# The residual of one half row of the last pair, added on TensorE in PSUM instead of by the store

## Chip, cores and metric

The kernel runs on one core of a Trainium2 chip. The metric is the device time of one execution in microseconds, the median of several runs. Lower is better. All times below are in microseconds unless marked ns.

## What is computed

One decoder layer on a sequence of 1024 tokens of width 1024, in fp32: a token-mixing sub-layer (attention and a gated recurrence), then a squared-ReLU MLP of width 4096. The end of it is what matters here:

```python
    h = rmsnorm(x, pre_w_mlp[l]) * (1.0 + sc2) + sh2
    u = jnp.square(jax.nn.relu(h @ w_up[l]))
    x = x + g2 * rmsnorm(u @ w_down[l], post_w_mlp[l])
```

So each row of the output is the residual x plus a row of the down projection, times a gate row (g2 times the norm's weight), times one number per row, the reciprocal root of the row's mean square. That number is known only when both halves of the row are complete.

## The kernel before

The 1024 rows are eight blocks of 128 rows (`tb` 0 to 7), each of two halves of 512 columns. A tile is 128x512 fp32, 256 KB. In the token-mixing part `out_proj` (L1045) computes the residual of the second sub-layer and stores it from GpSimd's queue (L1066). Thirteen of its sixteen tiles go straight into the output tensor `out`; three go to a scratch tensor in HBM, `x1d` (L1041), which the table `hold` (L1042) lists: block 3's second half and both halves of block 7.

Both MLP products are done in a block scheme with seven products per group instead of eight, each as three products of split fp32 operands. In the down projection a list of loads, `seq`, is worked through in order: `load_ahead` (L1320) issues loads some entries ahead from SyncE's queue, and `take` (L1327) hands out the next tile. The last three entries of `seq` are the residual tiles in `x1d` (L1318).

The last group of the down projection runs by row blocks `t` = 0 to 3, each of which completes two blocks of rows, t and t + 4. The loop over `order` (L1628) does t = 0, 1, 2 and the first three products of t = 3. Work on finished blocks is put off by some steps with `on` and done a step at a time: `square` (ScalarE squares a half with a running sum), `gated` (VectorE times the gate row), `root` (VectorE adds the two sums, GpSimd takes the power -0.5, tile `rrf`), `scaled` (ScalarE times that number, first the half `1 - half`, then `half`) and `onto_x` (L1619). The last is an adding store: GpSimd issues a DMA with `accum_op=add`, which adds the tile `acc` to what `out` holds, half 0 first. When a pair's second half is done, `half` is 0, so the scaling goes over half 1 and then half 0. Every engine works its own queue in the order in which the code records; a wait holds all that stands behind it on that engine.

`last_rows` (L1660) does what is left of t = 3: block a = 3 and block b = 7. TensorE's products go to the PSUM banks `pdlb`, `pdc`, `pda` and, last, `pdlx` in two parts of 256 columns. Block a's halves are multiplied by the gate row early (tiles `ga0` for half 0 and `ga` for half 1, L1686). After that:

- the root of block a (L1696), and for block b the sums, three squares (`finl`), the sum of them (`l_part`) and the root (`l_r`) on GpSimd
- `ga0`: scaled by block a's root on ScalarE (L1701) and stored by GpSimd as an adding store (L1706)
- `ga`: one VectorE instruction (times the root, plus the residual tile) and a plain store from SyncE (L1710)
- `gl` for both halves of block b: a VectorE instruction each and a plain store, from ScalarE's queue for half 0 and SyncE's for half 1 (L1713)

The program ends with a drain of each engine and a barrier, which the profile puts on L1781. All recorded operations pass through one helper and stand under L39.

Of the kernel before, what the change touches and what calls it, by code (L numbers as in the profile page):

```python
# [9 lines left out]
F32 = mybir.dt.float32  # L10
F32R = mybir.dt.float32r
I32 = mybir.dt.int32
AF = mybir.ActivationFunctionType
ALU = mybir.AluOpType
AX = mybir.AxisListType

P = 128
D = 1024
# [29 lines left out]
def hybrid_layer(ctx: ExitStack, tc: tile.TileContext, I, out, dbg=None):  # L48
    nc = tc.nc
    ACT, DVE, POOL, PE, SP = (Queue(tc, e) for e in (nc.scalar, nc.vector, nc.gpsimd, nc.tensor, nc.sync))  # L50
# [17 lines left out]
    small = ctx.enter_context(tc.tile_pool(name="small", bufs=2, side="right"))  # L68
# [3 lines left out]
    dram = ctx.enter_context(tc.tile_pool(name="dram", bufs=1, space=bass.MemoryType.DRAM))  # L72
# [19 lines left out]
    def tp_ps(name):  # L92
        return pb.tile([P, 512], F32, tag="b", name=name)

    def a_ps(name):
        return pa.tile([P, 512], F32, tag="aps", name=name)
# [18 lines left out]
    ident, cT, bT, prew1, prew2 = (tab[:, a:b] for a, b in ((0, P), (P, 136), (136, 184), (184, 192), (192, 200)))  # L115
# [922 lines left out]

    x2ctx = ExitStack()
    X2 = x2ctx.enter_context(tc.tile_pool(name="poolX2", bufs=1))  # L1040
    x1d = dram.tile([P, 3 * 512], F32, tag="x1d", name="x1d")  # L1041
    hold = {(3, 1): slice(0, 512), (7, 0): slice(512, D), (7, 1): slice(D, D + 512)}  # L1042
    xn2 = [None] * TB

    def out_proj(tb):  # L1045
# [106 lines left out]
    def flush():  # L1152
        for dst, src in pend:
            SP.dma_start(dst, src)
        pend.clear()
# [154 lines left out]
    for i, (g, n) in enumerate(stages):  # L1310
# [3 lines left out]
        if 10 <= i and gates:  # L1314
            entry_gate(*gates.pop(0))
        ends.append(len(seq))
    for i in range(3):
        seq.append((f"x1_{i}", lambda i=i: x1d[:, i * 512:i * 512 + 512], None))  # L1318

    def load_ahead():  # L1320
        while at["load"] < min(len(seq), at["use"] + (LEAD if at["load"] >= 16 else 4) + 1):
            k = at["load"]
            mk = (raw_, t_)[k % 2] if k < 16 else (raw_, t_, t_, raw_, t_, raw_, t_, t_)[k % 8]
            rawt[k] = load_raw(mk, seq[k][0], seq[k][1]())
            at["load"] += 1

    def take():  # L1327
        load_ahead()
        raw = rawt.pop(at["use"])
        at["use"] += 1  # L1330
        return raw

    def pump(count, limit=None):

        for _ in range(count):
            if at["use"] < (ends[-1] if limit is None else limit):
                k = at["use"]
                seq[k][2](take())
# [164 lines left out]
    def dmm(pst, g, n, t, first, cols=slice(0, 512)):  # L1503
        ps = GROUPS[g]
        for p in ps:
            (ah, al), (bh, bl) = (tuple(u[:, t * P:t * P + P] for u in su[p, n]), tuple(w[:, cols] for w in sw[p, n]))
            for x, (l, r) in enumerate(((ah, bh), (ah, bl), (al, bh))):
                PE.matmul(pst, lhsT=l, rhs=r, start=(first and p == ps[0] and x == 0), stop=(p == ps[-1] and x == 2),
                          skip_group_check=not first)

    def accum(tb, half, pst):
        if accs[tb][half] is None:
            accs[tb][half] = g_(f"acc{tb}_{half}")
            ACT.activation(accs[tb][half], pst, AF.Copy)
        else:
            DVE.tensor_tensor(accs[tb][half], pst, accs[tb][half], ALU.add)
# [77 lines left out]
    ssr, rr_, later = {}, {}, {}  # L1594

    def on(step, fn):
        later.setdefault(step, []).append(fn)

    def square(tb, half):
        if tb not in ssr:  # L1600
            ssr[tb] = small.tile([P, 2], F32, tag="ssf", name=f"ssf2{tb}")
        ACT.activation(a_ps(f"fin{tb}_{half}"), accs[tb][half], AF.Square, accum_out=ssr[tb][:, half:half + 1])

    def gated(tb, half):
        DVE.tensor_tensor(accs[tb][half], accs[tb][half], gw2[:, half * 512:half * 512 + 512], ALU.mult)
# [6 lines left out]
    def root(tb):  # L1612
        ss, rr_[tb] = (small.tile([P, 1], F32, tag=f"{n}1", name=f"{n}f{tb}") for n in ("ss", "rr"))
        root_of(rr_[tb], ss, ssr[tb][:, 0:1], ssr[tb][:, 1:2])

    def scaled(tb, half):
        ACT.activation(accs[tb][half], accs[tb][half], AF.Copy, scale=rr_[tb][:, 0:1])

    def onto_x(tb, halves=(0, 1)):  # L1619

        for half in halves:
            POOL.dma_start(out[tb * P:(tb + 1) * P, half * 512:half * 512 + 512], accs[tb][half], accum_op=ALU.add)
# [4 lines left out]
    bk = {}  # L1627
    for step, (_, t, k) in enumerate(order):  # L1628
        n = ORDER[k]
        key, first, th, half = PLAN[n]  # L1630
        flush()
        if first:
            bk[key, t] = (mm_ps if key == "a" else tp_ps)(f"pd{key}{g}_{t}")
        dmm(bk[key, t], g, n, t, first)
        while todo:
            todo.pop(0)()
        todo.append(lambda tb=t + 4 * th, half=half, pst=bk[key, t]: accum(tb, half, pst))
        for fn in later.pop(step, []):
            fn()
        if 2 <= step < 6:  # L1640
            pump(1)
        if k >= 3 and t < 3:
            tb = t + 4 * th
            on(step + 1, lambda tb=tb, half=half: square(tb, half))
            if k < 5:
                on(step + 3, lambda tb=tb, half=half: gated(tb, half))
            else:
                on(step + 3, lambda tb=tb: root(tb))
                on(step + 3, lambda tb=tb, half=half: gated(tb, half))
                for hf in (1 - half, half):  # L1650
                    on(step + 4, lambda tb=tb, hf=hf: scaled(tb, hf))
                on(step + 5, lambda tb=tb: onto_x(tb))
    nstep = len(order)

    def rest(step):
# [4 lines left out]
    def last_rows():  # L1660
        a, b, t = 3, 7, 3
        ss = small.tile([P, 3], F32, tag="ssl", bufs=1, name="ssl")
        one = {n: small.tile([P, 1], F32, tag="l_" + n, bufs=1, name="l_" + n) for n in ("part", "r")}
        h = [slice(0, 512), slice(512, D)]
        ba, bc, bb, bx = bk["a", 3], bk["c", 3], tp_ps("pdlb"), tp_ps("pdlx")
        gl = [m_(f"gl{half}") for half in range(2)]
        ga0, ga = m_("ga0"), m_("ga")

        def sq(acc, col, w=512):
            ACT.activation(a_ps("finl" + str(len(ssr)))[:, 0:w], acc, AF.Square, accum_out=col)  # L1670

        def add(dst, pst):
            DVE.tensor_tensor(dst, pst, dst, ALU.add)

        dmm(bb, g, 2, t, True)
        while todo:
            todo.pop(0)()
        rest(nstep)
        dmm(bc, g, 3, t, False)
        add(accs[a][0], bb)  # L1680
        square(a, 0)
        rest(nstep + 1)
        dmm(ba, g, 7, t, False)
        add(accs[a][1], bc)
        square(a, 1)
        DVE.tensor_tensor(ga0, accs[a][0], gw2[:, h[0]], ALU.mult)  # L1686
        DVE.tensor_tensor(ga, accs[a][1], gw2[:, h[1]], ALU.mult)
        rest(nstep + 2)
        acp = [accs[b][0][:, 256 * i:256 * i + 256] for i in range(2)]
        dmm(bx[:, 0:256], g, 4, t, True, slice(0, 256))  # L1690
        dmm(bx[:, 256:512], g, 4, t, True, slice(256, 512))
        for step in sorted(later):
            rest(step)
        add(accs[b][1], ba)
        sq(accs[b][1], ss[:, 0:1])
        root(a)  # L1696
        add(accs[b][0], ba)
        for i in range(2):
            add(acp[i], bx[:, 256 * i:256 * i + 256])
            sq(acp[i], ss[:, 1 + i:2 + i], 256)  # L1700
        ACT.activation(ga0, ga0, AF.Copy, scale=rr_[a][:, 0:1])  # L1701
        DVE.tensor_tensor(gl[1], accs[b][1], gw2[:, h[1]], ALU.mult)
        DVE.tensor_scalar(one["part"], ss[:, 0:1], ss[:, 1:2], D * EPS, ALU.add, ALU.add)
        DVE.tensor_tensor(one["part"], one["part"], ss[:, 2:3], ALU.add)
        POOL.tensor_tensor(one["r"], one["part"], mhalf[:, 0:1], ALU.pow)
        POOL.dma_start(out[a * P:(a + 1) * P, h[0]], ga0, accum_op=ALU.add)  # L1706
        DVE.tensor_tensor(gl[0], accs[b][0], gw2[:, h[0]], ALU.mult)
        xa, xl = take(), [take() for _ in range(2)]
        DVE.scalar_tensor_tensor(ga, ga, rr_[a][:, 0:1], xa, ALU.mult, ALU.add)
        nc.sync.dma_start(out[a * P:(a + 1) * P, h[1]], ga)  # L1710
        for half in range(2):
            DVE.scalar_tensor_tensor(gl[half], gl[half], one["r"][:, 0:1], xl[half], ALU.mult, ALU.add)
            (nc.sync if half else nc.scalar).dma_start(out[b * P:(b + 1) * P, h[half]], gl[half])  # L1713
# [71 lines left out]
```

## Time and profile before

| | us |
|---|---|
| runs before: median (lowest to highest of 3) | 1095.6 (1095.07 to 1096.14) |
| the profiled execution, its own time | 1095.36 |
| its span, first to last instruction | 1093.6 |
| TensorE busy | 1071.9 (98%) |
| VectorE busy | 801.2 (73%) |
| ScalarE busy | 585.4 (54%) |
| GpSimd busy | 373.9 (34%) |
| mean granted TensorE clock | 0.996 |

The span is what the profile covers; the execution's own time has 1.76 us around it. Instants are counted from the start of the span. PE is TensorE, DVE VectorE, ACT ScalarE, POOL GpSimd, SP SyncE; a q behind an engine's name marks its sequencer, which issues DMAs and waits. A row in order of time has its start, its length, the engine, the line, the operation and `out<-in` by tile names; what stands in brackets is the idle time before it and what ended that. DMA queue q0 is GpSimd's, q1 SyncE's and q10 ScalarE's; their shares are of the time of 16 DMA engines.

### The profile page before, as it was taken

Reading aid. Unit: us, or ns where it says so; the run is one execution under the profiler, and the core shown is the slowest. Engines: PE = TensorE matmul, PEld = TensorE weight load, DVE = VectorE, ACT = ScalarE, POOL = GpSimd, SP = SyncE. Lnnn points to the kernel's source line nnn. Section 1 sums busy time; section 2 is a strip of 40 time slices with the busy share of each in tenths; the row PEclk is TensorE's granted clock in tenths of the full one; section 3 lists DMA queues with packets and bytes.
Section 4 is the critical chain, followed back from the end, with each engine's and each line's share of the span. In section 5 each row is a group of like instructions: output and inputs, shape, how many; then the busy total and the mean of one; then the engine's idle time right before and its main releaser. Section 6 shows DMA issues by size and latency. Waiting matters only on the chain.

```text
span 1093.6 us, 16105 instructions
## 1 busy us (share of the span) xinstructions
PE 1071.9 (98%) x5483; PEld 875.9 (80%) x5483; DVE 801.2 (73%) x1339; ACT 585.4 (54%) x1206; POOL 373.9 (34%) x499
## 2 busy tenths in 40 slices
PE   8999999999999999999999999999999999999995
PEld 6888666788888888888888888888888888888884
DVE  4866768878865564559767767676777787899876
ACT  4535553454555754565655555555763543456434
POOL 1163211143234653433544334344333333310014
PEclk9999999999999999999999999999999999999998
DMA  9701202544310252423676776767998897998537
GB/s 351 270 19 60 96 1 58 166 126 126 116 59 30 88 198 82 135 92 131 195 257 231 239 260 221 262 220 261 342 346 273 274 300 256 332 307 277 170 79 131
DMA packets 101586, 203.37 MB, mean 186 GB/s; under 512 B 13024, under 2 KB 13680, under 8 KB 101504
## 3 DMA queue, kind: packets, MB, share of 16 engines
q1 hardware_dynamic: 85968, 154.52, 42.0%
q0 software_dynamic: 15392, 47.57, 14.7%
q8 instruction: 43, 0.70, 0.3%
q14 instruction: 39, 0.32, 0.1%
q10 hardware_dynamic: 144, 0.26, 0.1%
HBM read 147.25 MB, written 55.05 MB: 185 GB/s over the span
## 4 chain that ended last, share of the span: by engine, by line
PE 90%; DVE 3%; DMA 2%; ACT 2%; POOL 1%; issue 1%; SPq 0%; DVEq 0%; POOLq 0%; ACTq 0%
PE pda L39 16%; PE pua L39 14%; PE pdc L39 8%; PE po L39 8%; PE puc L39 7%; PE phg L39 4%; PE pu L39 4%; PE pdb L39 4%; PE phq L39 3%; PE pub L39 3%; PE phf L39 3%; PE pq L39 3%; PE pv L39 3%; PE pk L39 2%; PE o L39 1%; DMA wa<-wada 1%
## 5 line engine op out<-in xcount | busy, mean ns | idle before, releaser
L39 POOL TENSOR_TENSOR b<-b,b 128x512 f32<-128x512 f32 x64 | 89.2, 1393 | 223.3 <-DMA b<-w_dn 223.0
L39 ACT ACTIVATE dw<-dwr 128x512 fp32r<-128x512 f32 x72 | 45.4, 630 | 48.5 <-DMA dwr<-td 28.8
L39 ACT ACTIVATE s<-s 128x512 f32<-128x512 f32 x84 | 52.9, 631 | 32.4 <-DVE s L39 31.1
L39 DVE TENSOR_TENSOR dw<-dwr,dw 128x512 fp32r<-128x512 f32 x72 | 55.3, 769 | 4.5 <-ACT dw L39 4.5
L39 DVE TENSOR_TENSOR acc<-pda,acc 128x512 f32<-128x512 f32 x68 | 46.5, 684 | 15.4 <-PE pda L39 15.0
L39 POOL DMA_DIRECT2D td<-b x64 | 36.4, 569 | 21.6 <-POOL b L39 18.7
L39 ACT ACTIVATE s<-pua 128x512 f32<-128x512 f32 x28 | 16.7, 597 | 41.4 <-PE pua L39 35.9
L39 POOL TENSOR_TENSOR rrf<-ssf,mhalf 128x1 f32<-128x1 f32 x7 | 7.0, 1017 | 92.7 <-DVE ssf L39 92.7
L39 DVE TENSOR_TENSOR wt<-s,wt 128x512 fp32r<-128x512 f32 x42 | 36.9, 878 | 2.2 <-ACT wt L39 2.1
L39 ACT ACT_TABLE_LOAD x28 | 35.9, 1283 | 1.2 <-PEq L1778 0.7
L39 DVE SCALAR_TENSOR_TENSOR macc<-wada,cs,macc 128x512 f32<-128x512 f32 x42 | 33.4, 794 | 2.7 <-DMA wada<-wada 2.2
L39 POOL DMA_DIRECT2D b<-w_dn x64 | 34.5, 542 | 0.0
L39 DVE TENSOR_TENSOR wt<-a,wt 128x512 fp32r<-128x512 f32 x42 | 32.9, 784 | 0.9 <-ACT wt L39 0.9
L39 POOL TENSOR_TENSOR comb<-comb,rd 128x512 f32<-128x512 f32 x8 | 11.7, 1459 | 63.3 <-DVE rd L39 44.2
L39 PE MATMUL pua<-bt_0h,wt 128*128 128x512 f32 x84 | 32.7, 389 | 0.0
L39 PE MATMUL pua<-bt_1h,wt 128*128 128x512 f32 x84 | 32.7, 389 | 0.0
L39 PE MATMUL pua<-bt_2h,wt 128*128 128x512 f32 x84 | 32.7, 389 | 0.0
L39 PE MATMUL pua<-bt_3h,wt 128*128 128x512 f32 x84 | 32.7, 389 | 0.0
L39 DVE TENSOR_TENSOR acc<-pdc,acc 128x512 f32<-128x512 f32 x36 | 24.7, 685 | 9.2 <-PE pdc L39 9.0
L39 DVE TENSOR_TENSOR s<-puc,s 128x512 f32<-128x512 f32 x14 | 9.7, 690 | 29.0 <-issue 26.5
L39 ACT ACTIVATE wt<-s 128x512 fp32r<-128x512 f32 x42 | 26.3, 626 | 7.0 <-DVE s L39 6.8
L39 PE MATMUL pda<-dw,du_6h 128*128 128x512 f32 x96 | 29.5, 389 | 0.0
(763 smaller groups left out, 3762.7 us busy)
## 6 DMA issues: line engine op xcount, KB each, us to landing
dur<-ud SPq DMA_DIRECT2D x112, 256.0 KB, 4.3
wada<-wada SPq DMA_DIRECT2D x64, 256.0 KB, 3.6
b<-w_dn POOLq DMA_DIRECT2D x64, 256.0 KB, 5.1
td<-b POOLq DMA_DIRECT2D x64, 256.0 KB, 3.3
dwr<-td SPq DMA_DIRECT2D x64, 256.0 KB, 4.0
a<-w_u SPq DMA_DIRECT2D x56, 256.0 KB, 4.4
dwr<-w_dn SPq DMA_DIRECT2D x48, 256.0 KB, 4.8
ud<-s SPq DMA_DIRECT2D x42, 256.0 KB, 3.3
```

The source lines that it names most:

```text
L39: ins = op(*args, **kw)
```

## The change

The first half of block 3 is stored in another way. Its residual tile goes to `x1d` too, which now has four tiles and is loaded as four entries of `seq`. The four tiles are taken ahead of the last steps. A new PSUM bank `pdly` gets two fp32 products on TensorE: the identity times the residual tile, then a diagonal matrix `dg`, which ScalarE makes from the identity and block a's root, times the gated tile `ga0`. The second adds onto the first, so the bank holds the finished half row. ScalarE copies it back into `ga0`, and SyncE stores that with a plain store. Besides, `onto_x` gets the halves in the order in which they are scaled.

```diff
-    x1d = dram.tile([P, 3 * 512], F32, tag="x1d", name="x1d")
-    hold = {(3, 1): slice(0, 512), (7, 0): slice(512, D), (7, 1): slice(D, D + 512)}
+    x1d = dram.tile([P, 4 * 512], F32, tag="x1d", name="x1d")
+    hold = {(tb, half): slice(1024 * i + 512 * half, 1024 * i + 512 * half + 512)
+            for i, tb in enumerate((3, 7)) for half in range(2)}
...
-    for i in range(3):
+    for i in range(4):
         seq.append((f"x1_{i}", lambda i=i: x1d[:, i * 512:i * 512 + 512], None))
...
-                on(step + 5, lambda tb=tb: onto_x(tb))
+                on(step + 5, lambda tb=tb, half=half: onto_x(tb, (1 - half, half)))
...
-        ba, bc, bb, bx = bk["a", 3], bk["c", 3], tp_ps("pdlb"), tp_ps("pdlx")
+        ba, bc, bb, bx, by = bk["a", 3], bk["c", 3], tp_ps("pdlb"), tp_ps("pdlx"), tp_ps("pdly")
+        dg3 = small.tile([P, P], F32, tag="dg", bufs=1, name="dg3")
...
         dmm(bx[:, 256:512], g, 4, t, True, slice(256, 512))
+        xs = [take() for _ in range(4)]
+        PE.matmul(by, lhsT=ident, rhs=xs[0], start=True, stop=False)
...
         root(a)
         add(accs[b][0], ba)
+        ACT.activation(dg3, ident, AF.Copy, scale=rr_[a][:, 0:1])
+        PE.matmul(by, lhsT=dg3, rhs=ga0, start=False, stop=True)
...
-        ACT.activation(ga0, ga0, AF.Copy, scale=rr_[a][:, 0:1])
+        ACT.activation(ga0, by, AF.Copy)
...
-        POOL.dma_start(out[a * P:(a + 1) * P, h[0]], ga0, accum_op=ALU.add)
+        nc.sync.dma_start(out[a * P:(a + 1) * P, h[0]], ga0)
...
-        xa, xl = take(), [take() for _ in range(2)]
+        xa, xl = xs[1], xs[2:]
```

Two places show what this does to the queues. On ScalarE, the end of the program before (`fin` and `finl` are squares with a running sum, `rrf` is a block's root, `ga` the tile `ga0`):

```order
928 L39 ACTIVATE fin_0_10919,ssf_10918<-acc_0_8082 128x512
929 L39 ACTIVATE fin_1_10930,ssf_10918<-acc_1_8309 128x512
930 L39 ACTIVATE finl_10947,ssl<-acc_1_8189 128x512
931 L39 ACTIVATE finl_10955,ssl<-acc_0_8722 128x256
932 L39 ACTIVATE finl_10958,ssl<-acc_0_8722 128x256
933 L39 ACTIVATE ga_10898<-ga_10898,rrf_10950 128x512
934 L1713 DMA out<-gl_10896 128x512
```

and the same place after the change:

```order
928 L39 ACTIVATE fin_0_10923,ssf_10922<-acc_0_8082 128x512
929 L39 ACTIVATE fin_1_10934,ssf_10922<-acc_1_8309 128x512
930 L39 ACTIVATE finl_10952,ssl<-acc_1_8189 128x512
931 L39 ACTIVATE dg_10899<-c_tab,rrf_10955 128x128
932 L39 ACTIVATE finl_10962,ssl<-acc_0_8722 128x256
933 L39 ACTIVATE finl_10965,ssl<-acc_0_8722 128x256
934 L39 ACTIVATE ga_10902<-pdly 128x512
935 L1719 DMA out<-gl_10900 128x512
```

The diagonal stands between block b's first square and the two on 256 columns, and the scaling of `ga0` has become a copy from PSUM, at the same place.

On GpSimd, the end of the program before (`acc_1` and `acc_0` are the second and first halves of blocks 2 and 6, `ga` is `ga0`):

```order
481 L39 DMA out<-acc_0_8050 128x512
482 L39 DMA out<-acc_1_8267 128x512
483 L39 DMA out<-acc_0_8695 128x512
484 L39 DMA out<-acc_1_8163 128x512
485 L39 TENSOR_TENSOR rrf_10950<-ssf_10949,mhalf 128x1
486 L39 TENSOR_TENSOR l_r<-l_part,mhalf 128x1
487 L39 DMA out<-ga_10898 128x512
```

and after it:

```order
481 L39 DMA out<-acc_1_8267 128x512
482 L39 DMA out<-acc_0_8050 128x512
483 L39 DMA out<-acc_1_8163 128x512
484 L39 DMA out<-acc_0_8695 128x512
485 L39 TENSOR_TENSOR rrf_10955<-ssf_10954,mhalf 128x1
486 L39 TENSOR_TENSOR l_r<-l_part,mhalf 128x1
```

The halves of each pair of stores have changed places, here and in the pairs before, and GpSimd's last instruction is now a root, with no store behind it. The store of `ga0` stands on SyncE's queue, ahead of the one of `ga`.

## The prediction

> **What bounds the kernel now.** I read the page's chain first, then the last stretch by windows, by rows in order of time, by the instructions of the program's last line and by DMA queue. The chain by engine:
>
> ```profile
> PE 90%; DVE 3%; DMA 2%; ACT 2%; POOL 1%; issue 1%; SPq 0%; DVEq 0%; POOLq 0%; ACTq 0%
> ```
>
> TensorE sets the time until its last product; the change touches nothing ahead of that but the order of some stores. So the question is what lies between the last product and the end. Three windows of the tail (columns: length, busy time of PE, its weight loads, DVE, ACT, POOL, then granted clock, DMA share, GB/s):
>
> ```profile
> 1080.00:1085.70 5.70, 0.40 (x4) 0.20 (x2) 5.09 (x12) 2.35 (x7) 2.94 (x4) 0.86 1.07 189
> 1085.70:1090.00 4.30, 0.00 (x0) 0.00 (x0) 0.00 (x0) 0.00 (x0) 0.00 (x0) 0.50 0.80 206
> 1090.00:1093.60 3.60, 0.00 (x0) 0.00 (x0) 0.00 (x0) 0.00 (x0) 0.00 (x0) 0.50 0.00 0
> ```
>
> TensorE is busy for 0.40 us more and then done, at 1080.4. Until 1085.7 VectorE works nearly throughout (5.09 of 5.70) and the DMA engines are full; then 4.3 us hold transfers alone; the last 3.6 us hold neither work nor transfers. What ends there is in the rows of the program's last line (count, shortest/median/longest in ns, first and last start):
>
> ```profile
> L1781 POOLq DRAIN  x3: 46/108/9377, 1083.4 to 1093.3; - x3
> L1781 SPq DRAIN  x3: 7/7/7, 1090.4 to 1093.1; - x3
> L1781 PEldq DRAIN  x2: 13/1495/2977, 1077.5 to 1093.1; - x2
> L1781 DVEq DRAIN  x2: 19/802/1584, 1083.8 to 1093.1; - x2
> ```
>
> Each engine's first drain lasts until that engine has nothing under way: TensorE's from 1077.5 for 2.98 us, to 1080.45, where its matmuls end; VectorE's from 1083.8 for 1.58, to 1085.4. GpSimd's starts at 1083.4 and lasts 9.377 us, to 1092.8. SyncE's comes at 1090.4, when the last landing has been awaited. So for 2.4 us (1090.4 to 1092.8) everything waits for GpSimd's drain; from there the barrier and the end take 0.8 (to 1093.6). What GpSimd still has under way is seen in the last rows in order of time:
>
> ```profile
> 1082.44 0.71 ACT L39 ACTIVATE ga<-ga,rrf 128x512 f32<-128x512 f32 x1
> 1082.57 0.16 DVE L39 TENSOR_TENSOR l_part<-l_part,ssl 128x1 f32<-128x1 f32 x1
> 1082.64 0.69 DVE L39 TENSOR_TENSOR gl<-acc,gw 128x512 f32<-128x512 f32 x1
> 1082.81 0.93 POOL L39 TENSOR_TENSOR l_r<-l_part,mhalf 128x1 f32<-128x1 f32 x1 [1.65 <-DVE l_part L39]
> 1083.24 0.75 DVE L39 SCALAR_TENSOR_TENSOR ga<-ga,rrf,x 128x512 f32<-128x512 f32 x1
> 1083.70 0.89 POOL L39 DMA_DIRECT2D out<-ga  x1
> 1083.91 1.41 DVE L39 SCALAR_TENSOR_TENSOR gl<-gl,l_r,x 128x512 f32<-128x512 f32 x2
> 1084.02 0.34 SPq L1710 DMA_DIRECT2D out<-ga  x1
> 1084.69 0.37 ACTq L1713 DMA_DIRECT2D out<-gl  x1
> 1085.35 0.34 SPq L1713 DMA_DIRECT2D out<-gl  x1
> ```
> ```profile
> q0 software_dynamic: 1872, 3.41, 61.9%
> q1 hardware_dynamic: 288, 0.52, 3.8%
> ...
> out<-acc POOLq DMA_DIRECT2D x12, 256.0 KB, 5.5
> out<-ga POOLq DMA_DIRECT2D x1, 256.0 KB, 5.9
> out<-ga SPq DMA_DIRECT2D x1, 256.0 KB, 5.4
> out<-gl ACTq DMA_DIRECT2D x1, 256.0 KB, 5.2
> out<-gl SPq DMA_DIRECT2D x1, 256.0 KB, 4.8
> ```
>
> GpSimd's last instruction ahead of the drain is the adding store of ga0, issued at 1083.70, landed 5.9 later at 1089.6; the drain ends 3.2 us behind that landing. The last landing of all is SyncE's: 1085.35 + 4.8 = 1090.15. The queue rows cover 1055 to 1094 (39 us): q0 holds the 13 adding stores (12 and the one of ga0), 0.619 x 39 / 13 = 1.86 us of all 16 engines each; q1 the two plain stores of SyncE, 0.038 x 39 / 2 = 0.74. An adding store costs 2.5 plain ones.
>
> **The change, part by part.**
>
> *Four residual loads instead of three, taken before the last rows.*
>
> ```profile
> 1039.00 2.12 SPq L39 DMA_DIRECT2D x<-x1d  x3
> ```
>
> The three loads are issued 40 us ahead of use; a fourth behind them on SyncE's idle queue is some 0.7 us of issue (2.12 / 3), at nothing. Its cover would have to shrink by over 30 us to cost.
>
> *Two fp32 products behind the last matmul.* The nearest rows are earlier fp32 products with 512 columns, each of them two records, two products side by side in each row:
>
> ```profile
> 191.31 1.09 PE L39 MATMUL oT<-pp,kv 128*64 128x512 f32 x4
> 192.22 1.03 PE L39 MATMUL oT<-pc,kv 128*64 128x512 f32 x4
> ```
>
> One group follows the other after 0.91 us and lasts 1.03 to its end. The product with the identity needs only a residual that landed long ago: from about 1080.3 to 1081.3. The one with the diagonal needs the diagonal, which ScalarE makes once the row's root is there:
>
> ```profile
> 1077.00 3.58 POOL L39 DMA_DIRECT2D out<-acc  x4 [0.81 <-ACT acc L39]
> 1080.35 0.81 POOL L39 TENSOR_TENSOR rrf<-ssf,mhalf 128x1 f32<-128x1 f32 x1
> ```
> ```profile
> 1075.36 2.56 ACT L39 ACTIVATE acc<-acc,rrf 128x512 f32<-128x512 f32 x4 [1.34 <-POOL rrf L39]
> ...
> 1080.77 0.19 ACT L39 ACTIVATION_READ_ACCUMULATOR finl<-acc 128x1 f32 x1
> 1081.49 0.39 ACT L39 ACTIVATE finl<-acc 128x256 f32<-128x256 f32 x1 [0.53 <-DVE acc L39]
> ```
> ```profile
> L39 ACT ACTIVATE mxh<-sg 128x128 fp32r<-128x128 f32 x20 | 4.6, 310 | 0.0
> ```
>
> The root ends at 1081.16; a 128x128 ScalarE pass takes about 0.31, so the diagonal is there at 1081.5. It lies in a hole of ScalarE, which waits for VectorE from 1080.96 to 1081.49: it costs between nothing and 0.05 us. I take nothing. The second product then runs 1081.5 to 1082.6. Below nothing is excluded, since TensorE had no other work here.
>
> *ScalarE evacuates PSUM instead of scaling ga0.*
>
> ```profile
> L39 ACT ACTIVATE s<-pua 128x512 f32<-128x512 f32 x28 | 16.7, 597 | 41.4 <-PE pua L39 35.9
> ```
>
> 0.60 in place of 0.71, from 1082.6 instead of 1082.44, done at 1083.2 as before. ScalarE's next is the store at 1084.69: nothing. What stands behind the wait on TensorE is that store alone.
>
> *The store of ga0 goes from GpSimd to SyncE, plain.* On SyncE it can issue at about 1083.25; its 0.34 is over before the next one, at 1084.02. VectorE's rows stay as they are, so the last store still issues at 1085.35. On the DMA engines 1.86 becomes 0.74.
>
> *Adding stores in scaling order.* Each pair's first store no longer waits for the pair's second scaling: 2.56 / 4 = 0.64 us earlier. The stream of adding stores, full from 1080 on, ends about 0.6 earlier. Its last store, and that store's time to landing:
>
> ```profile
> 1078.76 1.81 POOL L39 DMA_DIRECT2D out<-acc  x1
> ```
> ```profile
> out<-acc POOLq DMA_DIRECT2D x1, 256.0 KB, 7.4
> ```
>
> It landed at 1078.76 + 7.4 = 1086.2; after the change, at 1085.6.
>
> *The sum.* Two paths to the end. GpSimd: its last transfer lands at 1085.6 instead of 1089.6; with the same 3.2 us behind it, the drain ends at 1088.8. SyncE: the transfers left after 1085.7 were 0.80 x 4.30 = 3.44 us of all engines and took 4.45 to the last landing. Now the adding store's 1.86 is out, of its plain copy's 0.74 all or nothing is done by then, and the rest starts 0.6 ahead: 1.0 to 1.7 left, which at 4.45 / 3.44 takes 1.3 to 2.2 us, to 1087.0 to 1087.9. A store without company has taken
>
> ```profile
> ud<-a SPq DMA_DIRECT2D x14, 256.0 KB, 2.4
> ```
>
> so 1085.35 + 2.4 = 1087.75 is the early bound, 1090.15 the late one. I take 1088.3, near the work's count, and 0.3 as before to SyncE's drain: 1088.6. The later path is 1088.8, plus 0.8: a span of 1089.6 against 1093.6. That is 4.0 us less. The profiled execution took 1095.36, 0.24 under the median of the runs (1095.6); off the median, 4.0 gives 1091.6. With the bounds of the last landing (span 1088.9 to 1091.2) and of the drain: 1090.6 to 1092.8.
>
> The Trainium skill (DMA: Bandwidth & Descriptors, Anatomy of one DMA) fits one transfer at 2.0 us plus its bytes at 436 GB/s, an estimate of 2.6 us for 256 KB; by it the last landing would be at 1087.95. No row of this tail is that short, since the transfers meet there.
>
> **The rivals.**
>
> *GpSimd's drain is a fixed cost of ending.* For it: it is one long row, and 9.4 us is longer than any transfer. Against: its other two are 46 and 108 ns, and the drains of TensorE and VectorE end with their work. If it lasted 9.38 from the issue of the last root (1082.85 instead of 1083.4), the end would come 0.6 sooner: 1095.0.
>
> *The drain goes, but the landings stay.* The same 256 KB still have to pass the same engines. Then SyncE's path holds: last landing 1090.15, drain 1090.4, end 1091.2, 2.4 less: 1093.2. Against: 1.86 against 0.74 for the same bytes. The Trainium skill (DMA: Bandwidth & Descriptors, Issuing engines are not separate DMA queues) says that another issuing engine saves the sequencer's time alone; by that rule this is the case, but this change also drops the addition.
>
> *Slower: the diagonal holds up ScalarE.* It stands in front of the last two squares and waits for GpSimd's root. If that ends after 1081.2, the squares, the last root, three stores and GpSimd's drain all shift by as much. A root that waits until the four adding stores' row is over (1077.00 + 3.58 = 1080.58, not 1080.35) and for one more issue of GpSimd (0.89) is 1.1 late. It decides only if the drain is fixed, from 0.6 us on: 1095.0 + 1.1 = 1096.1. For it: the root stands behind those stores on GpSimd. Against: they now leave earlier.
>
> **How the numbers follow.** Forecast 0.58, fixed drain 0.22, landings stay 0.15, late root 0.05. The bound of 0.2% (2.2 us, about what a measurement of this kernel can tell from no change) lies at 1093.4. Faster: 0.58 and 0.09 of the second rival, 0.67. Within: 0.22, 0.06 and 0.03, 0.31. Slower: 0.02. Forecast and second rival hold 0.73, so the range must reach the fixed drain: 1090.5 to 1095.2.
>
> **What would show it.** After: GpSimd's drain starts at about 1082.9 and ends near 1088.8, three us behind its last landing; the diagonal lies inside ScalarE's gap and VectorE ends at 1085.3 to 1085.4; q0 has 12 stores and is silent after 1085.6; the first store of each pair comes 0.6 after the first scaling begins. A drain of over 9 us, or a VectorE that ends after 1086, would make me wrong.

## The result, and the profile after

| | before | after |
|---|---|---|
| median of 20 runs each | 1095.14 us | 1093.05 us |
| lowest to highest | 1094.26 to 1096.82 | 1092.40 to 1094.75 |
| profiled execution | 1095.36 | 1093.02 |
| its span | 1093.6 | 1091.2 |
| its last product ends | 1080.40 | 1080.85 |
| from there to the end | 13.2 | 10.3 |

The ratio is 0.9978 (95%: 0.9972 to 0.9984), so about 2.4 us less (1.8 to 3.1); the two medians are 2.1 apart, inside that interval. The direction is as predicted and the time lies inside the overall range, but 4.0 us were forecast, and 1093.05 lies just outside the forecast's own range, 1090.6 to 1092.8. The last product (`pdlx`) ends at another time in each profile, between 1080.2 and 1082.1 over the kernels below, whatever was changed in the tail; so profiles are compared from that point, where this pair shows 2.9 less.

First the rows of the program's last line in the kernel after (shortest/median/longest in ns, first and last start):

```profile
L1787 POOLq DRAIN  x3: 46/99/7177, 1083.2 to 1090.9; - x3
L1787 SPq DRAIN  x3: 7/7/7, 1088.8 to 1090.7; - x3
L1787 PEldq DRAIN  x2: 13/594/1175, 1081.8 to 1090.7; - x2
L1787 DVEq DRAIN  x2: 19/802/1586, 1084.2 to 1090.7; - x2
```

GpSimd's long drain is 2.2 us shorter, 7.177 for 9.377, but it is still there, from 1083.2 to 1090.4. SyncE has awaited the last landing at 1088.8 and then waits 1.6 us for GpSimd. The windows (columns as before: length, busy time of PE, weight loads, DVE, ACT, POOL, granted clock, DMA share, GB/s) say the same:

```profile
1080.85:1086.20 5.35, 1.99 (x4) 0.33 (x3) 4.69 (x10) 2.56 (x8) 1.44 (x2) 0.98 1.01 208
1086.20:1088.80 2.60, 0.00 (x0) 0.00 (x0) 0.00 (x0) 0.00 (x0) 0.00 (x0) 0.50 0.61 236
1088.80:1091.20 2.40, 0.00 (x0) 0.00 (x0) 0.00 (x0) 0.00 (x0) 0.00 (x0) 0.50 0.00 0
```

The stretch with transfers alone has shrunk from 4.3 to 2.6; a stretch with neither work nor transfers remains, 2.4 long. GpSimd's rows in order of time, to its last instruction:

```profile
1075.59 0.93 POOL L39 TENSOR_TENSOR rrf<-ssf,mhalf 128x1 f32<-128x1 f32 x1 [0.40 <-DVE ssf L39]
1076.47 3.57 POOL L39 DMA_DIRECT2D out<-acc  x4
1080.80 0.56 POOL L39 TENSOR_TENSOR rrf<-ssf,mhalf 128x1 f32<-128x1 f32 x1 [0.76 <-DVE ssf L39]
1083.25 0.93 POOL L39 TENSOR_TENSOR l_r<-l_part,mhalf 128x1 f32<-128x1 f32 x1 [1.90 <-DVE l_part L39]
```

The last of the four adding stores alone, and its time to landing:

```profile
1078.18 1.86 POOL L39 DMA_DIRECT2D out<-acc  x1
...
out<-acc POOLq DMA_DIRECT2D x1, 256.0 KB, 7.9
```

It landed at 1078.18 + 7.9 = 1086.1. The drain ended 4.3 us behind that landing, where the kernel before showed 3.2, and 6.2 us behind the end of GpSimd's own last instruction, the root at 1083.25 + 0.93 = 1084.18. That is the question for the experiments. The queues from 1055 to 1094 (39 us):

```profile
q0 software_dynamic: 1728, 3.15, 57.0%
q1 hardware_dynamic: 432, 0.79, 5.3%
...
out<-acc POOLq DMA_DIRECT2D x12, 256.0 KB, 5.1
out<-ga SPq DMA_DIRECT2D x2, 256.0 KB, 3.3
out<-gl ACTq DMA_DIRECT2D x1, 256.0 KB, 3.4
out<-gl SPq DMA_DIRECT2D x1, 256.0 KB, 2.9
```

An adding store costs 0.570 x 39 / 12 = 1.85 us of 16 engines, a plain one of SyncE 0.053 x 39 / 3 = 0.69, as before. The four last stores land in 2.9 to 3.4 us instead of 4.8 to 5.9.

### The profile page after: what moved, and what is told of

Read it like the earlier page. It is cut to its first block, busy times and chain, and to the rows that moved or that the text cites. A ratio compares the mean times of both kernels' runs of the same rounds, so it can differ in the third digit from the quotient of the medians.

```text
span 1091.2 us, 16120 instructions
## 1 busy us (share of the span) xinstructions
PE 1074.9 (99%) x5487; PEld 877.0 (80%) x5487; DVE 807.6 (74%) x1339; ACT 585.7 (54%) x1207; POOL 372.8 (34%) x498
## 4 chain that ended last, share of the span: by engine, by line
PE 92%; DVE 3%; ACT 2%; DMA 1%; POOL 1%; issue 1%; SPq 0%; DVEq 0%; POOLq 0%; ACTq 0%
PE pda L39 16%; PE pua L39 14%; PE pdc L39 8%; PE po L39 8%; PE puc L39 7%; PE phg L39 4%; PE pu L39 4%; PE pdb L39 4%; PE pq L39 4%; PE phq L39 3%; PE pub L39 3%; PE phf L39 3%; PE pv L39 3%; PE pk L39 2%; PE o L39 1%; PE sc L39 1%
## 5 line engine op out<-in xcount | busy, mean ns | idle before, releaser
L39 POOL TENSOR_TENSOR comb<-comb,rd 128x512 f32<-128x512 f32 x8 | 11.7, 1458 | 63.3 <-DVE rd L39 44.3
L39 PE MATMUL pdc<-dw,du_3h 128*128 128x512 f32 x96 | 29.6, 389 | 0.0
L39 PE MATMUL pda<-dw,du_7h 128*128 128x512 f32 x96 | 29.6, 389 | 0.0
```

What stands on the lines that cost most here:

```text
L39: ins = op(*args, **kw)
```

## The experiments

What can hold GpSimd's drain? Two theories stood at first; the end of GpSimd's last instruction, store issues included, is called its own end here. **Landing**: it ends 3 us behind the landing of GpSimd's last transfer, as the prediction had it, and the landings were merely later than counted. **Own end**: it ends some 6.2 us behind GpSimd's last instruction, whatever it is. The experiments are edits of the kernel after, unless said otherwise. In the fences, the first number of a drain row's last part is the start of its longest drain.

**No adding stores of the last row of scalings (e1).**

```diff
-                on(step + 5, ... onto_x(tb, (1 - half, half)))
+                if t < 2:
+                    on(step + 5, ... onto_x(tb, (1 - half, half)))
```

> The changed kernel without the adding stores of blocks 2 and 6 (their MLP term is left out of the output). GpSimd's last store is then one of blocks 1 and 5, landed at about 1078.5. Theory 'landing': GpSimd's drain ends a fixed time (3.2 us before the change, 4.3 after it) behind the last landing of a GpSimd store, so here it ends with the last root, near 1084.2, and SyncE's drain at about 1088.5 sets the end: span about 1089.3, some 2 us under the changed kernel. Rival 'own end': the drain ends a fixed time behind GpSimd's last instruction (6.2 us behind the root l_r): 1090.4, span 1091.2, as in the changed kernel.

Measured: 1093.29, ratio to before 0.9981 (0.9972 to 0.9990), like the kernel after. Its drain, GpSimd's last instruction, its last two stores, and the later one's time to landing:

```profile
L1788 POOLq DRAIN  x3: 46/99/6851, 1084.5 to 1091.8; - x3
```
```profile
1084.51 0.93 POOL L39 TENSOR_TENSOR l_r<-l_part,mhalf 128x1 f32<-128x1 f32 x1 [1.91 <-DVE l_part L39]
...
1073.93 1.79 POOL L39 DMA_DIRECT2D out<-acc  x2 [1.05 <-ACT acc L39]
...
out<-acc POOLq DMA_DIRECT2D x1, 256.0 KB, 5.5
```

GpSimd's last transfer had landed at 1080.1, and the drain still lasted to 1091.3, 11.3 us behind it and 5.9 behind the root. Landing alone has fallen.

**No last root (e2).** GpSimd's last instruction is then block a's root, 2.7 us earlier.

```diff
-        POOL.tensor_tensor(one["r"], one["part"], mhalf[:, 0:1], ALU.pow)
...
-            DVE.scalar_tensor_tensor(gl[half], gl[half], one["r"][:, 0:1], ...)
+            DVE.scalar_tensor_tensor(gl[half], gl[half], rr_[a][:, 0:1], ...)
```

> The changed kernel without the last root l_r on GpSimd (block 7 is scaled with block 3's root instead). GpSimd's last instruction is then block 3's root, which ends at about 1081.4. Theory 'landing': the drain starts some 2 us sooner but ends where it did, 4.3 us behind the last landing of an adding store (1086.1): 1090.4, span 1091.2. Rival 'own end': 6.2 us behind 1081.4, that is 1087.6; SyncE's drain at about 1088.8 then sets the end, span 1089.6.

Measured: 1091.78, 0.9969 (0.9958 to 0.9981). Drains, then GpSimd's last instruction, its last store and that store's landing:

```profile
L1786 POOLq DRAIN  x3: 46/107/8112, 1080.9 to 1089.5; - x3
L1786 SPq DRAIN  x3: 7/7/7, 1088.7 to 1089.2; - x3
```
```profile
1080.91 0.56 POOL L39 TENSOR_TENSOR rrf<-ssf,mhalf 128x1 f32<-128x1 f32 x1 [0.75 <-DVE ssf L39]
...
1078.30 1.86 POOL L39 DMA_DIRECT2D out<-acc  x1
...
out<-acc POOLq DMA_DIRECT2D x1, 256.0 KB, 7.6
```

The own end moved to 1081.5, and 6.2 behind it would be 1087.7; the drain ended at 1089.0, 3.1 behind the landing at 1085.9. So own end alone has fallen too. What fits both is a third theory, **two terms**: the drain ends at the later of 6.2 us behind the own end (5.9 in e1, whose last landing lay far ahead of it) and 3.1 us behind the last landing. I took that for all the runs that follow.

**The store of ga0 plain, but from GpSimd (e3).**

```diff
-        nc.sync.dma_start(out[a * P:(a + 1) * P, h[0]], ga0)
+        POOL.dma_start(out[a * P:(a + 1) * P, h[0]], ga0)
```

> The changed kernel with the finished half row stored plainly by GpSimd instead of SyncE. Issue at about 1084.2, landing at about 1087.5. Theory 'landing': the drain ends 3.2 to 4.3 us behind that, 1090.7 to 1091.8, span 1091.5 to 1092.6. Rival 'own end': 8.2 us behind the end of GpSimd's last issue, as before the change: 1093.3, span 1094. A third view, that only an addition makes the drain long: the last addition is over at 1086.1 as in the changed kernel, so 1090.4 and a span of 1091.2.

Measured: 1093.24, 0.9981 (0.9972 to 0.9990).

```profile
L1787 POOLq DRAIN  x3: 46/99/7152, 1083.2 to 1090.9; - x3
```
```profile
1083.49 0.61 POOL L39 DMA_DIRECT2D out<-ga  x1
...
out<-ga POOLq DMA_DIRECT2D x1, 256.0 KB, 2.7
```

The store landed 2.7 us behind its issue, at 1086.2, and the drain ended at 1090.4, as in the kernel after. Counted from the last product, which ended at 1080.19 here, that is 10.2 us instead of 9.5: the own end is now the store's issue (1083.49 + 0.61 = 1084.1), 3.9 behind the last product instead of 3.3, and the drain ends 6.3 behind it. The medians are only 0.2 apart, which their intervals do not tell from nothing. So the one profile puts the change of engine at 0.6 us, through GpSimd's own end, and the medians do not show it. The Trainium skill (DMA: Bandwidth & Descriptors, Issuing engines are not separate DMA queues) says of the issuing engine that it saves no more than its sequencer's time; the two medians agree.

The store that no longer adds landed 6.0 behind the last product, where that of before landed 9.2 behind it (1089.6 - 1080.4). One profile of the order alone (e4, next) has 8.2, so not all of the 3.2 need be the addition's. The third view in the expectation, that only an addition makes the drain long, also gave 1090.4; e1 speaks against it, whose last addition was over at 1080.1 and whose drain still lasted 6.9 us.

**The order of the adding stores alone, in the kernel before (e4).**

```diff
-                on(step + 5, lambda tb=tb: onto_x(tb))
+                on(step + 5, lambda tb=tb, half=half: onto_x(tb, (1 - half, half)))
```

> The kernel before with the new order of the adding stores alone. Theory 'landing': the store of ga0 stays the last of GpSimd, at most 0.6 us sooner through the queue: 0 to 0.6 us less than before. Rival 'own end': the store's issue at 1083.7 is set by ScalarE, so nothing moves: 0.

Measured: 1094.49, 0.9994 (0.9985 to 1.0003), not told apart from no change; the interval goes from 1.6 us less to 0.3 more. Its drain ended at 1091.6, 3.2 behind the landing of `ga0` (1083.54 + 4.9 = 1088.4). In that one profile `ga0`'s store took 1.0 less to land than in before's (4.9 for 5.9); whether the order did that stays open.

**GpSimd's own end made later (e5).** A product that nobody reads behind the last root: no transfer, no landing, only a later own end.

```diff
         POOL.tensor_tensor(one["r"], one["part"], mhalf[:, 0:1], ALU.pow)
+        POOL.tensor_tensor(m_("idle"), gw2[:, h[0]], gw2[:, h[1]], ALU.mult)
```

> The changed kernel with one more GpSimd product of 128x512 (1.39 us in the profile of before) behind the last root; nothing reads its result. Theory 'two terms', from the runs so far: GpSimd's drain ends at the later of 5.9 to 6.3 us behind GpSimd's last instruction and 3.1 us behind the landing of its last transfer. So here the drain, and with it the span counted from the last product of the down projection, comes 1.3 to 1.4 us later than in the changed kernel. Rival 'landing': nothing moves, since no transfer does.

Measured: 1094.50, 0.9995 (0.9985 to 1.0004): the gain of the change is gone.

```profile
L1788 POOLq DRAIN  x3: 46/99/8547, 1083.1 to 1092.1; - x3
```
```profile
1083.09 0.93 POOL L39 TENSOR_TENSOR l_r<-l_part,mhalf 128x1 f32<-128x1 f32 x1 [1.90 <-DVE l_part L39]
1083.99 1.40 POOL L39 TENSOR_TENSOR idle<-gw 128x512 f32<-128x512 f32 x1
...
1084.19 2.41 DVE L39 SCALAR_TENSOR_TENSOR gl<-gl,l_r,x 128x512 f32<-128x512 f32 x2
```

The own end is at 1085.39 and the drain's at 1091.6, 6.2 behind it; the last landing, at 1085.3, was over by then, 6.3 back. From the last product to the end there are 11.7 us instead of 10.3: the 1.4 of the added product come out at the end in full. VectorE's last pair lasted 2.41 instead of 1.41 beside it, but that is not what was paid: SyncE's drain stood at 1088.7 all the same.

**The last root on ScalarE (e6).** It computes the same number in another way and takes the last instruction from GpSimd.

```diff
+        if step == 8:
+            ACT.activation(warm[:, 0:1], ones[:, 0:1], AF.Sqrt)
...
-        POOL.tensor_tensor(one["r"], one["part"], mhalf[:, 0:1], ALU.pow)
+        ACT.activation(one["r"], one["part"], AF.Sqrt)
...
+        DVE.reciprocal(one["r"], one["r"])
         for half in range(2):
```

> The changed kernel with the last root as a square root on ScalarE (its table loaded early, in an idle stretch) and a reciprocal on VectorE. GpSimd's last instruction is then block 3's root, at about 1081.4. 'Two terms': 6.2 behind it is 1087.6; 3.1 behind the last landing of an adding store (1086.1) is 1089.2, which sets the drain; SyncE's drain is at about 1088.9. Span 1.1 us under the changed kernel, some 3.3 under the kernel before (ratio about 0.997). Rival 'landing' with 4.3 us: no change against the changed kernel. Rival 'own end' alone: 1087.6, so SyncE's drain sets the end, 1.5 under the changed kernel.

Measured: 1091.75, 0.9969 (0.9959 to 0.9980), 1.3 us below the kernel after. The profiled execution was one of its longer ones (1092.96):

```profile
L1790 POOLq DRAIN  x3: 46/99/9660, 1080.7 to 1090.9; - x3
```
```profile
1078.18 1.85 POOL L39 DMA_DIRECT2D out<-acc  x1
...
out<-acc POOLq DMA_DIRECT2D x1, 256.0 KB, 9.1
```

The own end is now at 1081.3; the drain ended 9.1 behind it and 3.1 behind the last landing, 1087.3. That landing came 1.2 later than in the kernel after, though the store was issued at the same time; so this profile does not show the gain that the median shows. It was repeated as e12.

**The kernel after with the old order of the adding stores (e7).**

```diff
-                on(step + 5, lambda tb=tb, half=half: onto_x(tb, (1 - half, half)))
+                on(step + 5, lambda tb=tb: onto_x(tb))
```

> The changed kernel with the old order of the adding stores. 'Two terms': their last landing is up to 0.6 us later (1086.7), and 3.1 behind that is 1089.8, still ahead of the 1090.4 that GpSimd's last root gives: no difference from the changed kernel. Rival 'landing': up to 0.6 us longer than the changed kernel.

Measured: 1092.99, 0.9982 (0.9973 to 0.9991). Its last adding store landed at 1087.3, 1.2 later than in the kernel after, and its drain ended at 1090.4, as there: 6.4 behind the own end and 3.1 behind the landing, the two terms nearly level (6.2 behind the own end is 1090.2). The landing was 0.6 later than expected, but e6, with the new order, had one at 1087.3 too. The medians show nothing of the order here (1092.99 and 1093.05).

**The addition on VectorE instead of in PSUM (e8).** Both products, the diagonal and the copy are out; one VectorE instruction adds the residual, and SyncE's plain store stays.

```diff
-        PE.matmul(by, lhsT=ident, rhs=xs[0], start=True, stop=False)
...
-        ACT.activation(dg3, ident, AF.Copy, scale=rr_[a][:, 0:1])
-        PE.matmul(by, lhsT=dg3, rhs=ga0, start=False, stop=True)
...
-        ACT.activation(ga0, by, AF.Copy)
...
+        DVE.scalar_tensor_tensor(ga0, ga0, rr_[a][:, 0:1], xs[0], ALU.mult, ALU.add)
```

> The changed kernel without the two products, the diagonal and the copy: VectorE adds the residual in one instruction (0.75 us), as for the other half, and SyncE stores plainly. VectorE's end and SyncE's last landing come some 0.67 us later, to 1089.4, and SyncE's drain to 1089.5. 'Two terms': GpSimd's drain, 1090.4, stays the later one, so no difference from the changed kernel. Rival 'VectorE's chain': all of the 0.67 us is seen.

Measured: 1093.09, 0.9982 (0.9973 to 0.9991). VectorE ended 5.6 behind the last product instead of 4.9, and the drain at 1090.3, 6.2 behind the own end. SyncE's last landing, for which 0.67 was expected, came only 0.1 later behind the last product (8.0 for 7.9), since the last store landed in 2.4 us instead of 2.9; SyncE's path had 1.6 to spare in any case. The products in PSUM bring nothing here that one VectorE instruction would not.

**The root on ScalarE in the kernel before (e9).** The three edits of e6, made on before.

> The kernel before, with the last root on ScalarE and VectorE as in e6. GpSimd's last instruction is still the adding store of ga0. 'Two terms': the landing of that store (1089.6) plus 3.1 sets the drain, as before the change: no difference from the kernel before (within 0.4 us). Rival 'own end': the store no longer queues behind the root on GpSimd and is issued some 0.5 us sooner: 0.5 less.

Measured: 1094.83, 0.9998 (0.9989 to 1.0007).

```profile
L1784 POOLq DRAIN  x3: 46/99/8294, 1084.9 to 1093.7; - x3
```
```profile
1084.95 0.89 POOL L39 DMA_DIRECT2D out<-ga  x1 [2.29 <-ACT l_r L39]
...
out<-ga POOLq DMA_DIRECT2D x1, 256.0 KB, 5.1
```

There the landing, 1084.95 + 5.1 = 1090.1, holds the drain (3.1 behind it), and not the own end (the store's issue, ended at 1085.8). The same edit that gives 1.3 us after the change gives nothing before it that these runs tell from zero (0.2 less by the ratio, with an interval from 1.2 less to 0.8 more; 0.7 less by the medians).

**Both terms taken away (e10): e6 and e1 together.**

> e6 without the adding stores of blocks 2 and 6 (their MLP term is left out of the output). 'Two terms': GpSimd's last instruction ends at about 1081.4 and its last landing is at about 1079, so its drain is over by 1087.5, ahead of SyncE's at about 1088.7, which now sets the end: span 1089.5, counted from the last product (1080.8) 8.7 us, against 13.2 in the kernel before and 10.3 in the changed one. Rival: GpSimd's drain stays last for a reason that neither its own end nor its transfers give, and ends after SyncE's by more than 1 us.

Measured: 1090.51, 0.9953 (0.9940 to 0.9967).

```profile
L1791 POOLq DRAIN  x3: 46/108/6469, 1081.0 to 1088.9; - x3
L1791 SPq DRAIN  x3: 7/7/7, 1088.4 to 1088.7; - x3
```
```profile
1081.07 0.55 POOL L39 TENSOR_TENSOR rrf<-ssf,mhalf 128x1 f32<-128x1 f32 x1 [4.28 <-DVE ssf L39]
```

GpSimd's drain ends at 1087.5, 5.9 behind its own end (1081.6), and for the first time before SyncE's, at 1088.4. Now the landings of the plain stores set the end, and the program is over 8.1 us behind the last product. That is 0.6 less than the 8.7 expected: with the adding stores out, the last plain stores landed in 2.0 to 2.1 us.

**The kernel after and e6 once more, side by side (e11, e12).**

> The changed kernel once more, on the same chip as e12, so that the two can be set side by side. All theories: its ratio to the kernel before as measured, 0.9978 within its interval.

> The kernel of e6 once more, beside the changed kernel on the same chip. 'Two terms': GpSimd's drain is set by the landing of the last adding store plus 3.1 us, 0 to 1.1 us sooner than the changed kernel's 6.2 us behind the last root, by how late that landing falls; the median 0.5 to 1.3 us under e11's. Rival: the gain seen in e6 was the chip's, and the two agree within 0.3 us.

Measured: e11 1093.04 (1092.56 to 1094.23, 11 runs), 0.9979 (0.9971 to 0.9988); e12 1091.65 (1090.81 to 1091.99, 5 runs), 0.9964 (0.9951 to 0.9978). Every run of e12 lies below every run of e11. Drains of e12, its own end, its last store and that store's landing:

```profile
L1790 POOLq DRAIN  x3: 46/108/8368, 1081.0 to 1089.9; - x3
L1790 SPq DRAIN  x3: 7/7/7, 1089.0 to 1089.7; - x3
```
```profile
1081.07 0.56 POOL L39 TENSOR_TENSOR rrf<-ssf,mhalf 128x1 f32<-128x1 f32 x1 [0.76 <-DVE ssf L39]
...
1078.45 1.86 POOL L39 DMA_DIRECT2D out<-acc  x1
...
out<-acc POOLq DMA_DIRECT2D x1, 256.0 KB, 7.8
```

The landing at 1086.3 holds the drain (1089.4, 3.1 behind), 0.4 past SyncE's. This version beats both kernels: 3.6 per mille under before, 1.4 us under after.

All profiles against the two terms (drain end = first start plus longest drain; the term that decides in bold):

| kernel | own end | last own landing | drain's end | behind own end | behind landing |
|---|---|---|---|---|---|
| before | 1084.6 | 1089.6 | 1092.8 | 8.2 | **3.2** |
| after | 1084.2 | 1086.1 | 1090.4 | **6.2** | 4.3 |
| e1 | 1085.4 | 1080.1 | 1091.3 | **5.9** | 11.3 |
| e2 | 1081.5 | 1085.9 | 1089.0 | 7.5 | **3.1** |
| e3 | 1084.1 | 1086.2 | 1090.4 | **6.3** | 4.2 |
| e4 | 1084.4 | 1088.4 | 1091.6 | 7.2 | **3.2** |
| e5 | 1085.4 | 1085.3 | 1091.6 | **6.2** | 6.3 |
| e6 | 1081.3 | 1087.3 | 1090.4 | 9.1 | **3.1** |
| e7 | 1084.0 | 1087.3 | 1090.4 | 6.4 | **3.1** |
| e8 | 1084.0 | 1086.1 | 1090.3 | **6.2** | 4.2 |
| e9 | 1085.8 | 1090.1 | 1093.2 | 7.4 | **3.1** |
| e10 | 1081.6 | 1078.9 | 1087.5 | **5.9** | 8.6 |
| e11 | 1084.3 | 1086.0 | 1090.5 | **6.2** | 4.5 |
| e12 | 1081.6 | 1086.3 | 1089.4 | 7.8 | **3.1** |

In no row is the one below 5.9 or the other below 3.1, and in each row one of them is at its floor. e5 and e2 move the own end and the drain follows, in e2 as far as the landing lets it; e1 moves the landing alone, and counted from the last product only 0.3 follows (9.2 for 9.5). The ends of other engines do not explain the drain: in e8 VectorE ended 0.7 later and the drain did not move, and in e10 the drain was over before the last landings of the others.

## Why the prediction was right in direction and wrong in size

**The step that failed** is the one of the sum: "with the same 3.2 us behind it, the drain ends at 1088.8". That is 8.4 us behind the last product (1088.8 - 1080.40); it ended 9.55 behind it (1090.4 - 1080.85). The landing was as forecast, 5.2 us behind the last product (1085.6 - 1080.4) against 5.25 measured (partly by luck: in e6, with the same stores, it was 1087.3 - 1080.8 = 6.5), and the 3.2 us behind a landing are right wherever the landing decides (3.1 to 3.2 in seven profiles). But once the late landing was gone, a second term came up that the kernel before had hidden: 6.2 us behind the own end. In before the store's issue ended at 1084.6, which would have held the drain until 1090.8; the landing covered that by 2.0 us, to 1092.8. The change freed those 2.0, and 0.9 more because the own end went from the store back to the root ahead of it (0.89 of issue): 2.9, what the profiles show from the last product. The other 1.1 of the forecast 4.0 are the own end's. By the ratio of the runs the gap is 4.0 - 2.4 = 1.6, with the interval 0.9 to 2.2, which holds it. The prediction took a drain for a wait on things under way; the other engines' drains bore that out, but GpSimd's has a part that no transfer explains (e1). The sign named for being wrong, a drain of over 9 us, could not show this: the drain lasted 7.2.

**The range does not follow from its spans.** Spans of 1088.9 to 1091.2 against 1093.6 are 4.7 to 2.4 us less; off the median of 1095.6, from which the 1091.6 is counted, that is 1090.9 to 1093.2, not 1090.6 to 1092.8. Put so, 1093.05 lies inside, but near the bound at which no landing moves, which is not what happened.

**SyncE's path was right.** Forecast was a last landing at 1088.3, 7.9 behind the last product; it came at 1085.79 + 2.9 = 1088.7, 7.85 behind it (SyncE's last store is issued at 1085.79). Its drain, at 1088.8, has 1.6 to spare. The 1088.3 was picked between bounds of 1087.75 and 1090.15, above the 1087.0 to 1087.9 of the work's count, so the fit to 0.05 is luck. The Trainium skill (DMA: Bandwidth & Descriptors, Anatomy of one DMA) makes its fit for a DMA issued from GpSimd; the prediction's estimate from it, 2.6 us for 256 KB, is near the 2.7 of e3, the one plain store here that GpSimd issues. For SyncE's last store it lies under the 2.9 of the kernel after and above the 2.0 of e1, e5 and e10.

**The products were right.** TensorE and ScalarE in the kernel after, in order of time:

```profile
1080.57 0.28 PE L39 MATMUL pdlx<-dw,du_4l 128*128 128x256 f32 x1
1080.69 1.02 PE L39 MATMUL pdly<-x,c_tab 128*128 128x512 f32 x2
1081.85 1.13 PE L39 MATMUL pdly<-ga,dg 128*128 128x512 f32 x2
```
```profile
1081.22 0.19 ACT L39 ACTIVATION_READ_ACCUMULATOR finl<-acc 128x1 f32 x1
1081.39 0.40 ACT L39 ACTIVATE dg<-c_tab,rrf 128x128 f32<-128x128 f32 x1
1081.93 0.39 ACT L39 ACTIVATE finl<-acc 128x256 f32<-128x256 f32 x1
...
1083.01 0.60 ACT L39 ACTIVATE ga<-pdly 128x512 f32<-128x512 f32 x1
```

Each product takes 1.02 to 1.13 us (1.03 said), the copy 0.60. The diagonal took 0.40 instead of 0.31 and ended at 1081.79, inside ScalarE's hole: the next square starts 1.08 behind the last product, in before 1.09. The rival "late root" thus did not occur.

**The order of the stores was right in kind, and no run shows it to be worth anything.** The first store of the pair was issued 1.25 us behind the first scaling's start instead of 1.64: 0.4 gained, not the 0.64 counted, because it then stands behind the second of that step's two roots on GpSimd, until 1075.59 + 0.93 = 1076.52. And in the kernel after the own end holds the drain, not the landing that the order would make earlier; the median with the old order is the same (e7). In the kernel before, e4 leaves it open.

**The rivals.** "Landings stay" gave 1093.2, almost the measured time, but by a mechanism that isn't there: the last landing did move, from 1090.15 to 1088.7, further measured from the last product. Its number is right by coincidence. "Fixed drain" named half of what happened: there is a part of the drain that goes with GpSimd's last instruction. It is not the 9.4 us of the row, though, but a floor of 6.2, and so the end came 2.4 earlier, not 0.6.

**Where the rest of the gain lies.** In the kernel after, the own end holds the drain 1.1 us past what the landing would ask (1086.1 + 3.2 = 1089.3) and 1.6 past SyncE's. By the medians, taking the own end away gave 1.3 us (e2, e6) and 1.4 (e12); taking the landing away alone gave nothing (e1); both together gave 2.5 (1093.05 - 1090.51, e10), and then the landings of the plain stores set the end.

What the drain does inside its 6.2 us, why these are about twice the 3.1, and why they are 5.9 in e1 and e10, was not tried. Nor is it settled why the last adding store, issued 2.7 us ahead of the last product's end in e6 and in e12, landed 9.1 us later in the one and 7.8 in the other. The adding store of `ga0` scattered likewise: it took 5.9 us in the profile of before, 4.9 in e4 and 5.1 in e9. So part of the 4.0, and of the 2.9, may have rested on a profile with a late landing; one profile of each can't tell how much.

## What to carry to other kernels

At the end of a program look at each engine's drain and ask what it waits for, its transfers or its own last instruction: here GpSimd's last instruction had to end some 6 us, and its last landing some 3 us, ahead of SyncE's drain to cost nothing. When the wait that ends last is taken away, look for the next one in the same row before its whole length is counted as gain: here the hidden term lay only 2.0 us under the visible one and kept 1.1 of the forecast 4.0. And a store that adds costs some 2.5 plain ones in time of the DMA engines. Which engine adds the residual instead mattered nothing here (e8); which one issues the store made no difference that the medians show, though from GpSimd it makes the own end 0.6 us later (e3).

## What the runs showed of the hardware

GpSimd's drain has a floor of 5.9 to 6.3 us behind its last instruction, and one of 3.1 to 3.2 behind its last landing. The first holds in e1 and e10 too, where the last transfer had landed 5.3 and 2.8 us before that instruction ended (5.9 in both), and in e5, where it had landed 0.1 before (6.2). The drains of TensorE and VectorE show none such; they end with their work (in the kernel after at 1082.98 and 1085.8).

VectorE's pair of fp32 instructions went from 1.41 to 2.41 us beside a GpSimd product of 1.40 us (e5), while in the kernel after it starts 0.2 behind GpSimd's last root and overlaps no GpSimd work. The added 1.0 fell on the first of the two alone (1.75 for 0.75), which ended 0.55 behind the product. The Trainium skill (SBUF — State Buffer, SBUF: two separate sides) says that a VectorE instruction with two SBUF inputs and a GpSimd one that reads SBUF exclude each other on a shared port; the added 1.0 us agrees with that, though one run can't show the mechanism.
